# Hybrid attention layer: banded scores of two neighbouring pairs in one run, with the value sums in spare columns of the score tiles

## The chip, the cores and the metric

The kernel runs on one core of one Trainium2 chip. The metric is the device time of one execution in microseconds (us). A core has five engines that run their own instruction streams and wait for each other through semaphores: TensorE (PE; its weight loads are shown as PEld), VectorE (DVE), ScalarE (ACT), GpSimd (POOL) and SyncE (SP, which here only issues transfers). Matmul results go to PSUM, a small memory of eight banks. A bank holds 512 float32 columns in each of 128 partitions.

## The reference, cut to what matters

The reference is one decoder layer. A normalised input is projected to queries, keys, values and gates for two attention branches. Branch A is causal attention with a forget-gate bias over all 2048 positions. Branch B, the one that is changed here, is sliding-window attention with a window of 128 and a learned sink per head: eight query heads, two key/value heads, blocks of 128 queries. Each block sees the block of keys before its own and its own one.

```python
s = jnp.einsum('bnqhgd,bnshd->bnhgqs', qb, kk) * (d ** -0.5)
rel = i + Q_BLOCK - j
band = (rel >= 0) & (rel < WINDOW)
s = jnp.where(mask, s, -jnp.inf)          # mask = band, and no keys before block 0
p = jax.nn.softmax(jnp.concatenate([s, sink], axis=-1), axis=-1)[..., :-1]
out = jnp.einsum('bnhgqs,bnshd->bnqhgd', p, vv)
```

Both branches are gated, projected together, normalised and added to the residual. Inputs and output are float32, SEQ is 2048, D_MODEL 1024, a head 64 wide.

## The kernel before, in words

Every float32 product is made from float16 halves: a high and a low part on each side, and three matmuls (high·high, high·low, low·high) into the same PSUM columns.

The program has three long stages. First come the modulation, the normalised and transposed input and the first projections; then the banded branch B, which is worked off while the projections for both branches run; then branch A with the output projection. This case is about the second stage. Its PE stream is mostly projection matmuls, which are unit functions in a list (`punits`): three 512-column matmuls for a query or gate unit (L361), six 256-column ones for a value unit (L379). `fill(n)` emits the next n units.

Branch B has 32 `Pair` objects, the list `windows`: four pairs of heads (j) times eight pairs of query blocks (i = 0, 2, ... 14). They are called window 0 to 31 below. A pair goes through these parts:

- `scores` (L948): 12 matmuls on PE into a tile `pss` of two banks, one bank for each head. Each matmul contracts over 64 rows, half of the array; the two heads use the two halves. A bank has 256 columns for each of the two query blocks: 128 for the keys before, 128 for the block's own keys.
- `maxima` on DVE: L956 (COPY_PREDICATED) folds the first 128 columns of each 256 into the second 128, which works since within a band exactly one of the two is wanted at each place. L958 puts the sink into column 127. L961 and L963 make the row maximum and the bias.
- `exps` (L970): four exponentials on ACT, which read columns 127 to 255 of `pss`. After the fold, columns 0 to 126 of each 256 are read by nobody.
- `turn` (L977): four PE transposes into `pxb`; then L986 on ACT and L987 on DVE split the result into halves (`fold`), and four selections on POOL (L991, L993) unfold it into two weight tiles `ptb`.
- `pv` (L1005): 24 matmuls of 64 columns on PE (18 for i = 0), the sums of values, into a tile `pob` with a bank of its own. L1011 on DVE (`out_`) multiplies them by the reciprocal of the sums, and `o_store` sends them to memory.

The order in this stage is written by hand: every engine executes what the source calls, in the order of the calls. `after(k, f)` holds f back until the k-th `tick()` from there. Step n of the loop over windows reads: tick; maxima of window n; a quarter of the step's units; turn of window n-1; tick; exps of n; second quarter; tick; pv of n-2; third quarter; tick; last quarter; scores of n+1. A step is about 7.8 us. There is one `pss` buffer, so the scores of n+1 wait until the exps of n have read it.

PSUM in this stage: three banks `bk` for projections, two for `pss`, one for `pxb`, one for `pob`; the eighth is unused.

Of the kernel before, what the change touches and what calls it, by code (L numbers as in the profile page):

```python
# [10 lines left out]
F32 = mybir.dt.float32  # L11
# [5 lines left out]
ALU = mybir.AluOpType  # L17
AX = mybir.AxisListType

P = 128  # L20
# [4 lines left out]
CH = 512  # L25
# [18 lines left out]
def hybrid_layer(  # L44
# [17 lines left out]
    V, A, G, PE, SP = nc.vector, nc.scalar, nc.gpsimd, nc.tensor, nc.sync  # L62
# [5 lines left out]
    PSUM = bass.MemoryType.PSUM  # L68
# [14 lines left out]
    def sm(n, tag):  # L83
        return small.tile([P, n], F32, tag=tag, name=tag)
# [117 lines left out]
    def after(n, f):  # L202
        late.append([n, f])

    def tick():
        now = [f for n, f in late if n <= 1]
        late[:] = [[n - 1, f] for n, f in late if n > 1]
        for f in now:
            f()
# [85 lines left out]
    def o_store(on, pool, ci, rows_, cols_, eng, lag):  # L295
        if ci == 0:
            eng.dma_start(o_d[0][rows_, cols_].rearrange("(u p) c -> p u c", p=P), on)
            return
        u0, u1 = rows_.start // P, rows_.stop // P
        oh = pool.tile([P, u1 - u0, 2, on.shape[-1]], F16, tag="oh", name="oh")  # L300

        def low():
            V.tensor_tensor(oh[:, :, 1], on, oh[:, :, 0], op=ALU.subtract)
            eng.dma_start(o_d[ci][u0:u1, :, :, cols_].rearrange("u n p c -> p (u n) c"),
                          oh[:].rearrange("p u n c -> p (u n) c"))

        after(lag, lambda: A.activation(oh[:, :, 0], on, AF.Copy))
        after(lag + 1, low)
# [179 lines left out]
    with ExitStack():  # L488
# [114 lines left out]
        for _ in range(3):  # L603
            e = math.floor(math.log2(rest))
# [177 lines left out]
    def swa_pool(name, bufs, **kw):  # L782
        return swa.enter_context(tc.tile_pool(name=name, bufs=bufs, reuse_waits="tile", **kw))
# [148 lines left out]
    class Pair:  # L932
# [5 lines left out]
            self.blocks = [(i + e, max(i + e - 1, 0), 1 + min(i + e, 1)) for e in range(2)]  # L938

        def scores(self):  # L940
            self.pss = ps_s.tile([P, 2, CH], F32, tag="s", name="pss")
            q = ab[self.j, self.i // 4]
            for e, (i, k0, nk) in enumerate(self.blocks):
                qo, o = (i % 4) * P, e * 2 * P + (2 - nk) * P
                for n, (a, b) in enumerate(((0, 0), (0, 1), (1, 0))):
                    for h in range(2):
                        r = slice(64 * h, 64 * h + 64)
                        PE.matmul(self.pss[:, h, o:o + nk * P], q[r, a, qo:qo + P],  # L948
                                  kst[self.g][r, b, k0 * P:(i + 1) * P], start=(n == 0), stop=(n == 2))
# [45 lines left out]

            after(1, split)

        def pv(self):
            j, i = self.j, self.i
            po = ps_pv.tile([P, 4, 64], F32, tag="pv", name="pob")  # L1000
            for e, (i_, k0, nk) in enumerate(self.blocks):
                for h in range(2):
                    for b in range(nk):
                        for n, (pp_, vv) in enumerate(((0, 0), (0, 1), (1, 0))):
                            PE.matmul(po[:, 2 * e + h, :], self.ptt[b + 2 - nk][:, pp_, 2 * e + h, :],  # L1005
                                      vb[:, k0 + b, self.g, 64 * vv:64 * vv + 64],
                                      start=(b == 0 and n == 0), stop=(b == nk - 1 and n == 2))

            def out_():
                on = onp.tile([P, 2, P], F32, tag="on", name="on")  # L1010
                V.tensor_tensor(on[:].rearrange("p e (h d) -> p (e h) d", h=2), po[:],  # L1011
                                self.rinv[:].unsqueeze(2).broadcast_to([P, 4, 64]), op=ALU.mult)
                o_store(on[:], onp, i // 4, slice((i % 4) * P, (i % 4 + 2) * P), slice((4 + j) * P, (5 + j) * P), G, 1)

            after(1, out_)
# [166 lines left out]
    windows = [Pair(j, i) for j in range(4) for i in range(0, NB, 2)]  # L1182
    pos = [0]

    def fill(n, each=None):

        for _ in range(n):
            for f in events.pop(pos[0], []):
                f()
            punits[pos[0]]()  # L1190
            pos[0] += 1
            if each:
                each()
# [8 lines left out]
    with swa_order:  # L1202
        fill(N_PRO - 4, tick2)
        psx.close()
        sws = swa_pool("sws", 2)
        ptp = swa_pool("ptp", 1)
        ps_s = swa_pool("ps_s", 1, space=PSUM)
        ps_t = swa_pool("ps_t", 1, space=PSUM)
        ps_pv = swa_pool("ps_pv", 1, space=PSUM)
        wsp = swa_pool("wsp", 2)  # L1210
        wss, wst = sm(16, "a_m"), sm(2, "wst")
        wsq = {}
        base = N_PRO
        NW = len(windows)
        windows[0].scores()
        windows[0].maxima()
        fill(2, tick2)
        windows[0].exps()
        fill(2, tick2)
        for n, wd in enumerate(windows):  # L1220
            goal = base + (N_SWA - base) * (n + 1) // NW
            todo = goal - pos[0]
            part = [todo * (m + 1) // 4 - todo * m // 4 for m in range(4)]
            tick()
            if n:
                wd.maxima()
            fill(part[0])
            if n:
                windows[n - 1].turn()
            tick()  # L1230
            if n:
                wd.exps()
            fill(part[1])
            tick()
            if n > 1:
                windows[n - 2].pv()
            fill(part[2])
            tick()
            fill(part[3])
            if n + 1 < NW:  # L1240
                windows[n + 1].scores()

            if n:
                A.activation(wsq[n - 1][:], wsq[n - 1][:], AF.Square, accum_out=wss[:, (n - 1) % 16:(n - 1) % 16 + 1])
            if n == 16:
                V.tensor_reduce(wst[:, 0:1], wss[:], axis=AX.X, op=ALU.add)
            wsq[n] = wsp.tile([P, 2 * P], F32, tag="wsq", name="wsq")
            SP.dma_start(wsq[n][:], w_out0[n // 4 * P:(n // 4 + 1) * P, n % 4 * 2 * P:(n % 4 + 1) * 2 * P])
        tick()
        fill(5)  # L1250
        windows[NW - 1].turn()
        tick()
        fill(5)
        windows[NW - 2].pv()
        tick()
        fill(6)
        windows[NW - 1].pv()
        tick()
        tick()
        A.activation(wsq[NW - 1][:], wsq[NW - 1][:], AF.Square, accum_out=wss[:, 15:16])  # L1260
        V.tensor_reduce(wst[:, 1:2], wss[:], axis=AX.X, op=ALU.add)
        wsum = sm(1, "w_mx2")
        V.tensor_reduce(wsum[:], wst[:], axis=AX.X, op=ALU.add)
# [605 lines left out]
```

## Time and profile before

| | |
|---|---|
| median of three runs | 1130.42 us (1130.37 to 1131.12) |
| the profiled execution | 1129.92 us, its span from first to last instruction 1128.2 us |
| granted TensorE clock in it | 0.999 |
| PE matmuls busy | 1110.6 us, 98% of the span |
| DVE, ACT, POOL busy | 905.6, 656.8 and 224.6 us |
| scores of the 32 windows | first at 139.8 us, last at 378.9 us |

A matmul's busy time overlaps that of its neighbours, so two matmuls are compared by when they start. In the timeline a row merges instructions of one kind that follow each other: start, length from the first start to the last end, engine, line, operation, count; in square brackets stands the engine's idle time before the row and what ended it. A 512-column matmul takes 0.38 us from start to end, but the next one starts after 0.22 us. A view of windows gives the busy time of each engine in stretches of the span.

### The profile page before, as it was taken

To read this page: it belongs to the slowest core of one execution; us is meant where nothing else is said; L and a number is where in the kernel's file an instruction comes from. 1 tells how busy PE (TensorE), PEld (TensorE's weight loads), DVE (VectorE), ACT (ScalarE), POOL (GpSimd) and SP (SyncE) were. 2 spreads that over 40 slices of the span, in tenths; PEclk is the share of its full clock that TensorE was granted. 3 is DMA by queue.
4 is the path that set the end of the run, shared out by engine and by line. 5 is a ranking of instruction groups with operands and counts; after the bars stand their busy time and mean duration, and the time that the engine had idled before them with its cause. 6 is when DMAs were issued, how large, how long until landed. Compare 5 with 4: busy or idle time off the path is not lost.

```text
span 1128.2 us, 25138 instructions
## 1 busy us (share of the span) xinstructions
PE 1110.6 (98%) x9854; PEld 652.4 (58%) x9854; DVE 905.6 (80%) x1988; ACT 656.8 (58%) x1145; POOL 224.6 (20%) x343
## 2 busy tenths in 40 slices
PE   7899999999999999999999999999999999999997
PEld 2566555676756856556555555655556565544444
DVE  8897488878887468898998989988897997766663
ACT  3974345555555412666766667676666889543332
POOL 3111145545556420010010111001000000100000
PEclk9999999999999999999999999999999999999999
DMA  9854434413333142244223333224311245797632
GB/s 364 280 154 96 81 103 90 93 53 92 83 80 89 39 93 51 65 103 44 58 72 74 86 57 87 51 52 71 72 39 46 76 142 164 153 258 213 193 127 102
DMA packets 124653, 119.77 MB, mean 106 GB/s; under 512 B 66009, under 2 KB 102274, under 8 KB 124534
## 3 DMA queue, kind: packets, MB, share of 16 engines
q1 hardware_dynamic: 113662, 85.66, 28.4%
q0 software_dynamic: 10720, 32.46, 12.6%
q8 instruction: 77, 1.26, 0.6%
q14 instruction: 42, 0.34, 0.1%
q10 hardware_dynamic: 152, 0.04, 0.0%
HBM read 64.43 MB, written 25.18 MB: 79 GB/s over the span
## 4 chain that ended last, share of the span: by engine, by line
PE 83%; DVE 9%; DMA 3%; ACT 3%; issue 2%; SPq 0%; POOL 0%; DVEq 0%; POOLq 0%; ACTq 0%
PE bk L361 32%; PE bk L1650 14%; PE bk L379 7%; PE sta L1414 5%; PE sta L1415 5%; PE bk L1365 5%; PE poa L1440 3%; PE poa L1441 3%; PE poa L1438 3%; PE bk L854 2%; DMA wa<-in_w_ada_dram 2%; PE pss L948 2%; PE pob L1005 1%; PE px L453 1%; DMA xt<-in_x_dram 1%
## 5 line engine op out<-in xcount | busy, mean ns | idle before, releaser
L1421 ACT ACTIVATE p<-sta,lift,scl_qk 128x1024 f32<-128x1024 f32 (+2 forms) x160 | 171.8, 1074 | 128.1 <-PE sta L1415 78.9
L361 PE MATMUL bk<-hT,wh_qk 128*128 128x512 f16 x768 | 196.4, 378 | 0.0
L1428 DVE TENSOR_TENSOR pha<-p,pha 128x1024 f16<-128x1024 f32 (+2 forms) x160 | 168.9, 1056 | 0.2 <-ACT pha L1425 0.2
L1650 PE MATMUL bk<-wohl,oz 128*128 128x512 f16 x744 | 163.2, 379 | 0.0
L1368 DVE TENSOR_REDUCE a_m<-bk 128x1 f32<-128x512 f32 x192 | 130.1, 685 | 37.8 <-PE bk L1365 37.3
L1425 ACT ACTIVATE pha<-p 128x1024 f16<-128x1024 f32 (+2 forms) x160 | 147.8, 924 | 4.9 <-PE poa L1441 0.2
L1650 PEld LDWEIGHTS <-oz 128*128 128x128 f16 x744 | 71.0, 98 | 83.1
L1441 PE MATMUL poa<-vt,pha 128*128 128x65 f16 x1088 | 115.9, 192 | 0.7 <-DVE pha L1428 0.7
L1440 PE MATMUL poa<-vt,pha 128*128 128x64 f16 x1088 | 116.2, 194 | 0.0
L1438 PE MATMUL poa<-vt,pha 128*128 128x65 f16 x1088 | 116.2, 193 | 0.0
L361 PEld LDWEIGHTS <-wh_qk 128*128 128x128 f16 x768 | 71.8, 97 | 73.2 <-issue 1.3
L1414 PE MATMUL sta<-T 128*128 128x512 f16 (+1 forms) x320 | 110.9, 346 | 0.7 <-ACT p L1421 0.7
L1365 PE MATMUL bk<-T 66*128 66x512 f16 (+2 forms) x320 | 110.4, 348 | 0.5 <-DVE a_m L1368 0.2
L1415 PE MATMUL sta<-T 69*128 69x512 f16 (+1 forms) x320 | 109.8, 348 | 0.0
L1438 PEld LDWEIGHTS <-pha 128*128 128x128 f16 x1088 | 101.5, 96 | 14.3 <-issue 0.6
L1440 PEld LDWEIGHTS <-pha 128*128 128x128 f16 x1088 | 100.8, 97 | 11.4
L1441 PEld LDWEIGHTS <-pha 128*128 128x128 f16 x1088 | 100.9, 99 | 0.8 <-DVE pha L1428 0.8
L361 PE MATMUL bk<-hT,wh_za 128*128 128x512 f16 x384 | 100.4, 378 | 0.0
L361 PE MATMUL bk<-hT,wh_zb 128*128 128x512 f16 x384 | 92.1, 379 | 0.0
L379 PE MATMUL bk<-wh_va,hT 128*128 128x256 f16 x768 | 91.9, 273 | 0.0
L361 PE MATMUL bk<-hT,wh_qb 128*128 128x512 f16 x384 | 91.2, 379 | 0.0
L404 POOL DMA_DIRECT2D z_d<-tz x32 | 17.7, 555 | 342.5 <-DVE tz L402 250.9
(463 smaller groups left out, 1956.0 us busy)
## 6 DMA issues: line engine op xcount, KB each, us to landing
hT<-in_x_dram SPq DMA_DIRECT2D x20, 512.0 KB
wa<-in_w_ada_dram SPq DMA_DIRECT2D x16, 512.0 KB
z_d<-tz POOLq DMA_DIRECT2D x32, 256.0 KB, 3.1
T<-z_d SPq DMA_DIRECT2D x16, 512.0 KB
T<-stq SPq DMA_DIRECT2D x60, 128.0 KB
out_dram<-hT SPq DMA_DIRECT2D x15, 512.0 KB
xt<-in_x_dram SPq DMA_DIRECT2D x12, 512.0 KB
qs<-qf SPq DMA_DIRECT2D x80, 64.0 KB
```

The costliest lines, as they stand in the source:

```text
L361: PE.matmul(ps, whl[:, a, k, :], hT[ci][:, b, k, :], start=(k == 0 and n == 0), stop=(k == KT - 1 and n == 2))
L379: PE.matmul(ps[:, (u % 2) * 2 * P:(u % 2 + 1) * 2 * P], hT[ci][:, a, k, u * P:(u + 1) * P], wv[p][:, b, k, :], start=(k == 0 and n == 0), ...
L1365: PE.matmul(mx[:, :w], T[0:XM, 0, i * P:(i + 1) * P], T[0:XM, 2, pc * CH:pc * CH + w], start=True, stop=True)
L1414: PE.matmul(self.st[:, o:o + w], T[:, 3, kb_], T[:, 1, qc], start=True, stop=False)
L1415: PE.matmul(self.st[:, o:o + w], T[0:XR, 2, kb_], T[0:XR, 0, qc], start=False, stop=not diag)
L1421: A.activation(self.p32[:, :self.w], self.st[:, :self.w], AF.Exp, scale=scl[f"qk{self.hd}"][:], bias=lift[:])
L1425: A.activation(self.ph[:, 0, :self.w], self.p32[:, :self.w], AF.Copy)
L1428: V.tensor_tensor(self.ph[:, 1, :self.w], self.p32[:, :self.w], self.ph[:, 0, :self.w], op=ALU.subtract)
L1438: PE.matmul(po[:, u, :], ph[:, 0, pq], vt[:, b, hd, 0:65], start=(self.first and n == 0 and u == 0), stop=False)
L1440: PE.matmul(po[:, u, 0:64], ph[:, 0, pq], vt[:, b, hd, 65:VW], start=False, stop=False)
L1441: PE.matmul(po[:, u, :], ph[:, 1, pq], vt[:, b, hd, 0:65], start=False, stop=(self.last and n == len(self.blocks) - 1))
L1650: PE.matmul(py, self.hl[:, i, k, :], w_slot(8 * j + k)[:, cc], start=(k == 0 and m_ == 0), stop=(k == KT - 1 and m_ == 2))
```

## The change

There are two `pss` buffers, s0 and s1, of two banks each, and `pob` is gone: 3 + 4 + 1 banks, all eight. The windows take the buffers in the order s0, s1, s1, s0, s0, s1, s1, s0, and so on.

The scores of two windows are emitted together, 24 matmuls in one run: 0 and 1 before the loop, then n+1 and n+2 at the end of each odd step n. Even steps have no scores.

The value sums of window n-2 go to columns 0 to 63 of each 256 in a score tile ("home"). In an odd step this is the tile of window n-1, and `pv` stays where it was on PE but now stands ahead of the tick, so that `out_` comes a tick earlier. In an even step it is the tile of window n itself, and `pv` moves behind the third quarter of units. So the sums of windows n-2 and n-1 (n even) use the same tile one after the other, and the tile is next written by the scores of window n+3.

```diff
         def scores(self):
-            self.pss = ps_s.tile([P, 2, CH], F32, tag="s", name="pss")
+            self.pss = ps_s.tile([P, 2, CH], F32, tag=f"s{(self.i // 4 + self.i // 2) % 2}", name="pss")
...
-        def pv(self):
+        def pv(self, home):
             j, i = self.j, self.i
-            po = ps_pv.tile([P, 4, 64], F32, tag="pv", name="pob")
+            po = home.pss[:].rearrange("p h (e c) -> p e h c", e=2)[:, :, :, 0:64]
             for e, (i_, k0, nk) in enumerate(self.blocks):
...
-                            PE.matmul(po[:, 2 * e + h, :], self.ptt[b + 2 - nk][:, pp_, 2 * e + h, :],
+                            PE.matmul(po[:, e, h, :], self.ptt[b + 2 - nk][:, pp_, 2 * e + h, :],
...
             def out_():
                 on = onp.tile([P, 2, P], F32, tag="on", name="on")
-                V.tensor_tensor(on[:].rearrange("p e (h d) -> p (e h) d", h=2), po[:],
-                                self.rinv[:].unsqueeze(2).broadcast_to([P, 4, 64]), op=ALU.mult)
+                V.tensor_tensor(on[:].rearrange("p e (h d) -> p e h d", h=2), po,
+                                self.rinv[:].rearrange("p (e h) -> p e h", e=2).unsqueeze(3).broadcast_to([P, 2, 2, 64]),
+                                op=ALU.mult)
...
-        ps_pv = swa_pool("ps_pv", 1, space=PSUM)
...
         windows[0].scores()
+        windows[1].scores()
         windows[0].maxima()
...
             fill(part[1])
+            if n > 1 and n % 2:
+                windows[n - 2].pv(windows[n - 1])
             tick()
-            if n > 1:
-                windows[n - 2].pv()
             fill(part[2])
+            if n > 1 and n % 2 == 0:
+                windows[n - 2].pv(wd)
             tick()
             fill(part[3])
-            if n + 1 < NW:
-                windows[n + 1].scores()
+            if n % 2:
+                for wn in windows[n + 1:n + 3]:
+                    wn.scores()
...
-        windows[NW - 2].pv()
+        windows[NW - 2].pv(windows[NW - 2])
...
-        windows[NW - 1].pv()
+        windows[NW - 1].pv(windows[NW - 1])
```

Three places show how instructions move. The first is on PE at the end of step 3, where before the scores of window 4 end. L361 rows are projection units; in square brackets stand the engines whose semaphore is waited for. Before:

```order
L948 LDWEIGHTS stb
L948 MATMUL pss<-kst_576,stb 128x256
L361 LDWEIGHTS wh_qb_2115
L361 MATMUL bk_137<-hT_107,wh_qb_2115 128x512
L361 LDWEIGHTS wh_qb_2115
```

And with the change:

```order
L948 LDWEIGHTS stb
L948 MATMUL pss<-kst_576,stb 128x256
L948 LDWEIGHTS stb
L948 MATMUL pss<-kst_576,stb 128x256 [waits DVE_49]
L948 LDWEIGHTS stb
```

The scores of window 5 follow those of window 4 without a projection between. Their first matmul waits for DVE: for the L1011 of window 1, whose sums lie in the tile that window 5 now writes.

The second place is on PE in step 4, at the value sums of window 2 (weights `ptb`). Before:

```order
L361 LDWEIGHTS wh_qb_2115
L361 MATMUL bk_137<-hT_107,wh_qb_2115 128x512
L1005 LDWEIGHTS ptb [waits Pool_49]
L1005 MATMUL pob<-vb,ptb 128x64 [waits DVE_49]
L1005 LDWEIGHTS ptb
```

And with the change:

```order
L361 LDWEIGHTS wh_zb_1923
L361 MATMUL bk_139<-hT_108,wh_zb_1923 128x512
L1005 LDWEIGHTS ptb [waits DVE_49,Pool_49]
L1005 MATMUL pss<-vb,ptb 128x64 [waits Activation_49]
L1005 LDWEIGHTS ptb
```

Six L361 matmuls that stood behind the sums stand ahead of them. The first sum waits for ACT: for the last exponential of window 4, which reads the same tile. All even steps have this wait.

The third place is on DVE in step 5, around the L1011 of window 3. L285 is a weight split that waits for ACT; minus rows are of before, plus rows of the change:

```order
 L987 TENSOR_TENSOR fold<-pxb,fold 128x512
 L989 RECIPROCAL b_ri<-b_rs 128x4
-L285 SCALAR_TENSOR_TENSOR wh_va_2441<-wr_va_1990,w_sw,wh_va_2441 128x4x128
-L1011 TENSOR_TENSOR on<-pob,b_ri 128x256
-L285 SCALAR_TENSOR_TENSOR wh_va_2441<-wr_va_1990,w_sw,wh_va_2441 128x4x128
-L179 TENSOR_SCALAR kap_va_2490<-w_pw,pH 128x1
+L1011 TENSOR_TENSOR on<-pss,b_ri 128x256
+L285 SCALAR_TENSOR_TENSOR wh_va_2435<-wr_va_1987,w_sw,wh_va_2435 128x4x128 x2
+L179 TENSOR_SCALAR kap_va_2484<-w_pw,pH 128x1
+L303 TENSOR_TENSOR oh<-on,oh 128x2x128
```

L1011 now stands ahead of the first L285. In steps 7 and 9 it moves ahead of its neighbours in the same way; in step 3 it stays where it was. Behind the second stage the order of every engine is unchanged.

## The prediction

> **What bounds the kernel now.** I read the page first, then PE's timeline around one group of scores, then DVE and ACT at the places where the change puts waits.
>
> ```profile
> span 1128.2 us, 25138 instructions
> PE 1110.6 (98%) x9854; PEld 652.4 (58%) x9854; DVE 905.6 (80%) x1988; ACT 656.8 (58%) x1145; POOL 224.6 (20%) x343
> 160.00:170.00 10.00, 10.00 (x89) 5.34 (x85) 9.63 (x24) 4.73 (x14) 4.61 (x8) 1.00 0.31 89
> 170.00:180.00 10.00, 10.00 (x87) 5.24 (x86) 9.72 (x24) 5.67 (x21) 7.30 (x10) 1.00 0.45 107
> 240.00:250.00 10.00, 10.00 (x109) 7.47 (x106) 5.36 (x13) 4.37 (x15) 3.17 (x5) 1.00 0.18 53
> ```
>
> PE sets the end: 98% of the span, and 10.00 of 10 us in the windows of the banded stage. Whatever PE saves or waits there moves the rest of the program one for one, as PE has hardly any idle time later that could absorb it. The third number in a window row is DVE. It is full from 160 to 180 us (9.63, 9.72) and half empty at 240 us (5.36): a wait on DVE means different things early and late in the stage.
>
> **What merging the groups saves.** PE at the scores of window 4, from the merged timeline and from two narrow ones:
>
> ```profile
> 169.28 2.11 PE L361 MATMUL bk<-hT,wh_qb 128*128 128x512 f16 x9
> 171.32 0.83 PE L948 MATMUL pss<-kst,stb 64*128 64x256 f16 x12
> 171.32 0.39 PE L948 MATMUL pss<-kst,stb 64*128 64x256 f16 x4
> 171.66 0.49 PE L948 MATMUL pss<-kst,stb 64*128 64x256 f16 x6
> 172.08 1.47 PE L361 MATMUL bk<-hT,wh_qb 128*128 128x512 f16 x6
> 173.39 0.60 PE L977 MATMUL pxb<-ident,sm__2192 128*128 128x128 f32 x4
> ```
>
> Six L361 from 172.08 to 173.39 are 0.218 us apiece, so the nine from 169.28 would hand over at 171.23; the scores start at 171.32: entry costs about 0.10. The two heads of a pair run side by side. Four matmuls span 0.39 and six span 0.49, so a pair follows a pair after 0.10 to 0.11. The last of the three pairs from 171.66 then starts at about 171.87, and PE would go on at 171.98; L361 starts at 172.08: exit costs 0.10. A merged group drops one entry and one exit, 0.19 with the rounding. 32 groups become 16: **16 × 0.19 = 3.0 us saved**.
>
> Two groups waited besides:
>
> ```profile
> 206.34 2.75 PE L361 MATMUL bk<-hT,wh_zb 128*128 128x512 f16 x12
> 209.19 0.83 PE L948 MATMUL pss<-kst,stb 64*128 64x256 f16 x12
> 337.73 1.89 PE L361 MATMUL bk<-hT,wh_qb 128*128 128x512 f16 x8
> 339.73 0.83 PE L948 MATMUL pss<-kst,stb 64*128 64x256 f16 x12
> ```
>
> 12 × 0.216 from 206.34 and the entry give 209.03; the start at 209.19 is 0.16 late, at 339.73 likewise 0.17. The first is window 9, which now writes a tile that is free early: **0.16 saved**. The second is window 26, below. Matmuls, DVE, ACT and POOL instructions are otherwise the same in number and size, so they cost nothing more; one L1011 still reads 256 elements. SP's issues stand in the same order, and POOL only swaps five output stores with a neighbour; no engine waits for those stores in this stage.
>
> **New wait 1: window 5 on DVE's L1011 of window 1.** The chain on DVE that leads to it:
>
> ```profile
> 156.33 0.70 DVE L956 COPY_PREDICATED pss<-dmask,pss 128x512 f32<-128x512 int16 x1 [0.99 <-PE pss L948]
> 160.51 2.12 DVE L822 TENSOR_TENSOR qs<-qs,sinT 128x512 f32<-128x512 f32 x1
> 173.00 0.41 DVE L1011 TENSOR_TENSOR on<-pob,b_ri 128x256 f32<-128x256 f32 x1
> 184.78 0.17 DVE L989 RECIPROCAL b_ri<-b_rs 128x4 f32<-128x4 f32 x1
> 186.91 0.78 DVE L285 SCALAR_TENSOR_TENSOR wh_va<-wr_va,w_sw,wh_va 128x512 f16<-128x512 f32 x1 [1.97 <-ACT wh_va L278]
> 187.62 0.41 DVE L1011 TENSOR_TENSOR on<-pob,b_ri 128x256 f32<-128x256 f32 x1
> ```
>
> No row between 156.33 and 184.78 has idle time ahead of it: DVE works without a break. It starts when window 2's scores are there, now 0.19 earlier, so its L1011 ends at 173.41 - 0.19 = 173.22. PE gets to window 5 at 171.32 less two merges (0.38) plus window 4's six pairs (0.64): 171.58. **PE stands 1.6 us.** Behind it stand all projections, and nobody else has the work to fill. From below: if DVE loses L822's long 2.12 (a normal one is 0.69, see 191.19 in the next fence), 0.2. From above 2.1, if DVE is held again by the later turn.
>
> By the Trainium skill's page "SBUF — State Buffer" (section "SBUF: two separate sides"), a DVE instruction with two SBUF inputs and a GpSimd instruction lock each other out for the whole instruction. By that rule L822 is long since POOL's selections of window 1 run then; the trace agrees:
>
> ```profile
> 161.45 0.62 POOL L993 TENSOR_SCALAR_AFFINE_SELECT ptb<-fold 128x512 f16<-128x512 f16 x1
> 162.66 0.69 DVE L823 TENSOR_TENSOR qc<-qc,qs 128x512 f32<-128x512 f32 x1
> 191.19 0.69 DVE L822 TENSOR_TENSOR qs<-qs,sinT 128x512 f32<-128x512 f32 x1
> ```
>
> POOL's last selection ends at 162.07, and L822 at 162.63, one length later. The turn of window 1 moves behind window 3's scores, 0.45 later in all, and POOL with it, so I keep the long L822 and the 1.6.
>
> In steps 5, 7 and 9 the same wait (windows 7, 9, 11) finds DVE done: the L1011 moves ahead of L285, out of the ACT wait of 1.97, and runs near 185.4 instead of 187.62, while PE comes after 187. Later DVE has slack.
>
> **New wait 2: the sums of even steps on the exps of the same step.** First where PE leads, step 12:
>
> ```profile
> 234.70 0.60 PE L977 MATMUL pxb<-ident,sm__3165 128*128 128x128 f32 x4
> 235.14 1.46 PE L361 MATMUL bk<-hT,wh_qb 128*128 128x512 f16 x6
> 236.43 0.86 PE L1005 MATMUL pob<-vb,ptb 128*128 128x64 f16 x24
> 235.39 0.60 ACT L986 ACTIVATE fold<-pxb 128x512 f16<-128x512 f32 x1 [2.69 <-PE pxb L977]
> 235.88 0.45 ACT L970 ACTIVATE sm__3296<-pss,b_nb,scl_qb 128x129 f32<-128x129 f32 x1
> 237.53 0.22 ACT L970 ACTIVATION_READ_ACCUMULATOR sm__3296<-pss,b_nb,scl_qb 128x1 f32 x1
> ```
>
> ACT's exps stand behind L986, which waits for PE's turn at 234.70: they end at 237.75, 3.05 after it. The sums stood 1.73 after the turn; with six more L361 (1.30) they stand 3.03 after it. PE arrives 0.02 early, plus some 0.05 for the signal: 0.07 a step. About ten even steps from 10 to 30 are built like that: **0.7 us**; from 0 to 1.2.
>
> Early, where DVE is late, steps 4, 6 and 8:
>
> ```profile
> 177.93 0.21 ACT L970 ACTIVATION_READ_ACCUMULATOR sm__2311<-pss,b_nb,scl_qb 128x1 f32 x1
> 190.14 0.86 PE L1005 MATMUL pob<-vb,ptb 128*128 128x64 f16 x24
> 192.95 0.21 ACT L970 ACTIVATION_READ_ACCUMULATOR sm__2552<-pss,b_nb,scl_qb 128x1 f32 x1
> ```
>
> Step 6: PE at 190.14 + 1.30 (units) + 0.64 (window 7's scores, already done) - 0.57 (three merges) + 1.6 (the stall above) = 193.1; the exps end at 193.16 less what DVE gains. The stall above has paid for most of this; I take **0.5 us** for the three steps together, 0 to 1.9 if DVE in turn is held by the later sums.
>
> The Trainium skill, "PSUM — Partial Sum Buffer" (section "PSUM bank collisions raise a hardware error"), wants PSUM guarded by bank, not by address. That speaks against the change: the columns are free after the fold, yet their bank is busy until the exps have read it. The built order agrees, as the sums wait for ACT. If only the columns counted, this wait would end with DVE's fold and its 1.2 us would be 0.
>
> **Window 26.** DVE is full here again:
>
> ```profile
> 325.57 0.27 DVE L955 MEMSET pss<- 128x256 f32 x1 [1.62 <-PE pss L948]
> 339.47 0.20 ACT L970 ACTIVATION_READ_ACCUMULATOR sm__4947<-pss,b_nb,scl_qb 128x1 f32 x1
> ```
>
> From the start on window 24's scores, DVE and ACT need until 339.67 for the exps of 25, which window 26 waits for. PE cannot use its merge there: its 0.17 wait becomes 0.36, which costs **0.2** of what I booked as saved; 0 to 0.7.
>
> **Sum:** -3.0 - 0.16 + 1.6 + 0.7 + 0.5 + 0.2 = -0.2 us. The profiled execution took 1129.92 (1.7 outside its span), so 1129.7; the median of the runs is 0.5 above it: **1130.2 us**. With all waits at their lower ends (0.2, 0, 0, 0) it would be 1127.5; with all at their upper ends (2.1, 1.2, 1.9, 0.7) 1133.1.
>
> **Rivals.**
> - The gain stays (0.18). DVE reaches L1011 by 171.6, and the exps of steps 4 to 8 are earlier as well. Terms: -3.16 + 0.2 + 0.4 (half the 0.7) = -2.6, so 1127.8. For it: L1011 moves ahead in many steps, and L822's 1.4 us may go. Against it: without a stall at window 5, step 6's sums would meet exps that end 1.6 later than PE comes, so DVE would have to gain twice.
> - Slower (0.13). DVE executes in order, and L1011 of an even step is now called right behind sums that PE reaches about 2 us later than before. DVE then stands, and the next maxima, exps and scores are late. Before, the list of waits has it three times:
>
> ```profile
> DVE on L1011 <- PE pob L1005: 3.7, 3, 1.7
> ```
>
> In the seven even steps where DVE is full (4 to 10, 20, 24, 26), 0.7 each would be 4.9. Half of it in PE's way, on top of the sum, gives about 1132.7; it decides from about 0.7 a step. Against it: after the stall at window 5 DVE has slack.
> - The change does not save what it says (0.05): the 0.19 belongs to something else than the change of shape. Then +3.0 on the sum, 1133.2. Against it: entry and exit look the same at every group.
>
> **How the numbers follow.** My forecast, stalls eating nearly all of the gain, has 0.64, with its own range 1128.6 to 1131.9. A measurement of this kernel tells about 0.2% from no change, 2.3 us: faster is below 1128.2, slower above 1132.7. The first rival lies mostly beyond the one border, half of the second and most of the third beyond the other, and the forecast's own tails reach a little over both. Faster 0.19, same 0.68, slower 0.13. The range for 8 in 10 is 1128.0 to 1132.5.
>
> **What would show it.** The stage's end on PE before:
>
> ```profile
> 401.01 0.28 PE L1722 MATMUL bk<-w_mx,ones 128*128 128x1 f32 x2
> ```
>
> Right: 16 runs of 24 score matmuls, each with one entry and one exit; one PE wait of 1 to 2 us at about 171.6 on DVE L1011; waits of up to 0.1 on ACT L970 ahead of the sums of even steps; total PE matmul idle up by some 3 us in the stage. L1722 would come within 1 us of 401.01. Wrong: no wait at 171.6, or even-step waits of 0.3 and more after 230 us, or DVE rows of L1011 with a microsecond of idle time ahead of them.

## The result and the profile after

The change made the kernel slower: 1137.63 us median (1135.05 to 1139.78) against 1130.77 (1130.04 to 1131.81) for the kernel before on the same chip, a ratio of 1.0061 with a 95% interval of 1.0044 to 1.0077. That is 6.9 us, outside the range of the prediction. The profiled execution of the changed kernel, 1139.78 us, is the longest of its runs; the one of before, 1129.92 us, is shorter than each of the six of this comparison. So the profiles lie 9.9 us apart, 3.0 more than the medians.

Nearly all of it arises in the banded stage. The page of the changed kernel, two of its windows with one of before between them (columns as in the prediction: length, busy time of PE, PEld, DVE, ACT and POOL, granted clock, share of the transfer engines, GB/s), and PE's timeline with the first two long stalls, a merged run, and the end of the stage, which stood at 401.01 us before:

```profile
span 1138.1 us, 25131 instructions
PE 1111.5 (98%) x9854; PEld 655.9 (58%) x9854; DVE 905.1 (80%) x1988; ACT 656.9 (58%) x1145; POOL 221.9 (20%) x343
```

```profile
170.00:180.00 10.00, 8.49 (x80) 4.74 (x79) 8.79 (x22) 4.39 (x17) 7.28 (x10) 1.00 0.35 102
280.00:290.00 10.00, 10.00 (x109) 8.30 (x108) 7.04 (x20) 6.15 (x19) 5.82 (x9) 1.00 0.40 65
280.00:290.00 10.00, 8.60 (x86) 5.71 (x84) 5.99 (x12) 4.15 (x15) 5.20 (x9) 1.00 0.40 50
```

```profile
173.25 0.83 PE L948 MATMUL pss<-kst,stb 64*128 64x256 f16 x12 [1.51 <-DVE on L1011]
...
194.98 0.86 PE L1005 MATMUL pss<-vb,ptb 128*128 128x64 f16 x24 [1.59 <-ACT sm__2558 L970]
...
236.40 1.48 PE L948 MATMUL pss<-kst,stb 64*128 64x256 f16 x24
237.81 1.47 PE L361 MATMUL bk<-hT,wh_qb 128*128 128x512 f16 x6
...
410.24 0.28 PE L1726 MATMUL bk<-w_mx,ones 128*128 128x1 f32 x2
```

The stage ends 9.2 us later and the span is 9.9 longer; past the stage there is little to find. The merging is there as forecast: at 236.40 us 24 score matmuls stand in one row, with one entry and one exit. PE, which was full in these windows before (the middle row above and those of the prediction), is now idle for 1.5 us of 170 to 180 us and for 1.4 us of 280 to 290. What it waited for, from the list of PE's waits between 135 and 411 us (total, times, longest):

```profile
PE pss L1005 <- ACT sm__4329 L970: 2.3, 1, 2.3
PE pss L1005 <- ACT sm__2558 L970: 1.6, 1, 1.6
PE pss L948 <- DVE on L1011: 1.5, 1, 1.5
PE pss L1005 <- ACT sm__2805 L970: 1.4, 1, 1.4
PE pss L1005 <- ACT sm__4036 L970: 1.4, 1, 1.4
PE pss L948 <- ACT sm__4921 L970: 0.9, 1, 0.9
```

The kernel before has no row of PE in this list at all. Counted as start-to-start distance above the usual one, which includes the signal, these are: step 20 2.48 us, step 6 1.76, window 5 1.68, step 8 1.59, step 18 1.57, window 26 0.94. Eight even steps add 0.07 to 0.10 each, together 0.7, and two small ones (window 21, the sums in step 26) 0.6. Behind the longest stall PE ran 3.4 us at half its clock, which cost 1.35 us. The sum is some 12.6; less the 3.0 saved and the 0.34 that PE had stood before, 9.3, where the stage's end shows 9.2.

### The profile page after: what moved, and what is told of

It is laid out like the page before. It is cut to its first block, busy times and chain, and to the rows that moved or that the text cites. A ratio compares the mean times of both kernels' runs of the same rounds, so it can differ in the third digit from the quotient of the medians.

```text
span 1138.1 us, 25131 instructions
## 1 busy us (share of the span) xinstructions
PE 1111.5 (98%) x9854; PEld 655.9 (58%) x9854; DVE 905.1 (80%) x1988; ACT 656.9 (58%) x1145; POOL 221.9 (20%) x343
## 4 chain that ended last, share of the span: by engine, by line
PE 79%; DVE 9%; DMA 5%; ACT 3%; issue 3%; POOL 1%; SPq 0%; DVEq 0%; POOLq 0%; ACTq 0%
PE bk L361 31%; PE bk L1654 13%; PE bk L379 5%; PE sta L1418 5%; PE sta L1419 5%; PE bk L1369 4%; PE poa L1444 3%; PE poa L1445 3%; PE poa L1442 3%; PE bk L854 2%; DMA wa<-in_w_ada_dram 2%; PE pss L1005 1%; PE pss L948 1%; PE px L453 1%; DMA mxr<-mx_d 1%
## 5 line engine op out<-in xcount | busy, mean ns | idle before, releaser
L361 PE MATMUL bk<-hT,wh_qk 128*128 128x512 f16 x768 | 196.4, 378 | 0.0
L361 PEld LDWEIGHTS <-wh_qk 128*128 128x128 f16 x768 | 71.8, 97 | 73.2 <-issue 1.3
L361 PE MATMUL bk<-hT,wh_za 128*128 128x512 f16 x384 | 100.4, 378 | 0.0
L361 PE MATMUL bk<-hT,wh_qb 128*128 128x512 f16 x384 | 91.7, 384 | 0.0
L361 PE MATMUL bk<-hT,wh_zb 128*128 128x512 f16 x384 | 91.4, 379 | 0.0
```

Source lines behind the costliest of these rows:

```text
L361: PE.matmul(ps, whl[:, a, k, :], hT[ci][:, b, k, :], start=(k == 0 and n == 0), stop=(k == KT - 1 and n == 2))
```

## The experiments

The first theory: PE stands because sums of even steps now need the exps of the same step and window n+3's scores need an L1011. Its rivals: the merging itself costs; the late transfers that the second half of the profile shows (ACT's L1248 stands for 5.8 us there) are the cause, whatever PE waits for; DVE and ACT are simply the bound in these steps, so that a stall that is removed comes back elsewhere.

| kernel | median, us | ratio to before (95%) | stage's end in its profile, us | PE's extra gaps, us |
|---|---|---|---|---|
| changed kernel, again | 1136.25 | 1.0051 (1.0036 to 1.0065) | 406.78 | 9.1 |
| scores singly | 1140.94 | 1.0089 (1.0076 to 1.0102) | 412.40 | 11.7 |
| both sums in odd steps | 1135.79 | 1.0048 (1.0036 to 1.0060) | 408.77 | 10.6 |
| the same, window 5 alone | 1135.88 | 1.0038 (1.0026 to 1.0049) | 405.69 | 8.2 |
| sums in pairs | 1129.97 | 1.0000 (0.9991 to 1.0008) | 400.44 | 2.6 |
| the change without squares | 1134.32 | 1.0040 (1.0027 to 1.0053) | 404.81 | 7.5 |
| before without squares | 1130.32 | 0.9999 (0.9990 to 1.0008) | 401.00 | 0.4 |
| pairs, tiles in turn | 1129.52 | 0.9994 (0.9985 to 1.0003) | 399.85 | 2.1 |
| the same, scores singly | 1132.49 | 1.0018 (1.0009 to 1.0027) | 402.25 | 0.9 |
| pairs split by the turn | 1128.91 | 0.9985 (0.9976 to 0.9994) | 400.10 | 2.1 |

The last two columns are of one profiled execution each, which is not the median one (that of "both sums in odd steps" took 1138.61 us). The last column sums what the distances between PE's matmuls have above the usual ones, from 130 to 420 us; excesses below 0.06 us are not counted, those of matmuls at a low clock are (1.6 us in "scores singly", 2.8 in "both sums in odd steps", none in the others of the table). It is 12.6 in the first profile of the change and 0.3 in that of the kernel before.

**The changed kernel again.**

> The changed kernel once more, so that its stalls are seen in a second execution. Waits theory (PE stands at the sums of even steps, which now need the exps of the same step, and at window 5's scores, which need an L1011): the stalls of 1.7 us at window 5 and of about 1.7 us each at the sums of steps 6 and 8 return in every execution, and the time stays 4 to 9 us above the kernel before. Transfer theory (the loss is in late transfers of qs, wsq and mxr around 283 to 294 us, by accident of one execution): the stalls of steps 18 and 20 and the low clock at 307 us are gone here or stand elsewhere, and the time follows them by up to 5 us.

Measured: 1136.25 us. Window 5 (1.68), step 6 (1.75) and step 8 (1.59) are the same to 0.01 us, and so is window 26 (0.94). Steps 18 and 20 shrink from 1.57 and 2.48 to 1.1 each, and there is no low clock. So the first group belongs to the kernel, and what varies between executions are the transfers behind steps 18 and 20 and the clock.

**Scores singly.**

```diff
-        windows[1].scores()
...
-            if n % 2:
-                for wn in windows[n + 1:n + 3]:
-                    wn.scores()
+            if n + 1 < NW:
+                windows[n + 1].scores()
```

> Two tiles and the sums in their columns as in the change, but the scores of one window at the end of every step, as before. Waits theory: the 3.0 us of merging are lost, the stall of 1.7 us at window 5 goes, and the sums of even steps stand longer for it (steps 4, 6 and 8 together by 1 to 2 us more): 1137 to 1141 us. Rival, the merging itself costs (a group of 24 score matmuls holds PE while DVE waits for the maxima of the even window): without it the time falls back to 1130 to 1133 us.

Measured: 1140.94 us, in the range of the waits theory; the merging is not what costs. The stage ends 2.2 us later than in the first profile of the change (412.40 against 410.24), although PE's extra gaps are 0.9 smaller (11.7 against 12.6): without the merging 3.1 us are missing, as the prediction has it. With no stall at window 5, the sums of step 4 stand (first row; the second is step 6):

```profile
PE pss L1005 <- ACT sm__2306 L970: 1.3, 1, 1.3
PE pss L1005 <- ACT sm__2545 L970: 0.9, 1, 0.9
```

**Both sums in odd steps.** The sums of window n-3 stand at the start of odd step n, those of n-2 at their old place, both in the tile of n-1. The new second argument of `pv` is the first column of each 256.

```diff
+            if n > 2 and n % 2:
+                windows[n - 3].pv(windows[n - 1])
             tick()
...
-                windows[n - 2].pv(windows[n - 1])
+                windows[n - 2].pv(windows[n - 1], 64)
...
-            if n > 1 and n % 2 == 0:
-                windows[n - 2].pv(wd)
```

> As the change, but both sums of two steps in the odd step: those of window n-3 at its start and of n-2 at their old place, side by side in the free columns of window n-1, whose exps ended a step ago. Waits theory: the waits on L970 ahead of sums are gone (about 3.4 us at steps 6 and 8, 4.0 at 18 and 20, 0.7 of small ones), with them the low clock; window 5's 1.7 us stays, and some 0.3 and 0.9 us at windows 21 and 26: 1130.8 - 3.0 - 0.2 + 2.9 = 1130.5 us, 1129 to 1132. Transfer theory: the stalls around 287 and 305 us come whatever PE waits for, at another instruction: 1134 to 1137 us.

Measured: 1135.79 us. The first theory falls in its simple form: the waits of the even steps are gone, the loss is not. The sums in the next step still meet exps that are not done, and the second sums now wait for the L1011 of the first:

```profile
PE pss L1005 <- DVE on L1011: 2.9, 2, 2.2
PE pss L948 <- DVE on L1011: 1.9, 1, 1.9
PE pss L1005 <- ACT sm__2805 L970: 1.3, 1, 1.3
PE pss L1005 <- ACT sm__4329 L970: 1.0, 1, 1.0
```

The number is what the transfer theory gave, but of the five stalls behind these rows three (172, 212 and 340 us) are far from the late transfers.

**Window 5 alone.** In the last kernel, window 5 is scored at the end of step 4.

```diff
-                for wn in windows[n + 1:n + 3]:
+                for wn in windows[n + 1:n + 2 + (n != 3)]:
                     wn.scores()
+            if n == 4:
+                windows[5].scores()
```

> As the kernel with both sums in the odd step, and window 5's scores alone at the end of step 4, so that they need not wait for the L1011 of window 1. Waits theory: 1.7 us less of stall, one merge less (0.2): 1.5 us below the kernel with both sums in the odd step, so 1129.0 us, 1127.5 to 1130.5. Rival, the stall only paid for later ones (PE meets late exps or late maxima at windows 6 to 9 instead): no difference of more than 0.5 us between the two.

Measured: 1135.88 us, no better. The stall of 2.06 us that the kernel above has at window 5 is gone, and the sums of window 3 stand for 1.94 us in step 5 instead (from 181.66), for an L1011. This is the rival's case: as long as the next meeting of PE with DVE or ACT has as little slack, it takes over the stall.

**Sums in pairs.** The second theory: DVE and ACT run up to some 2.5 us behind in steps 4 to 9 and 18 to 26, also in the kernel before; PE stands wherever the order gives it less slack than that. So both sums go next to each other, with no L1011 between them, where the exps they need were called four quarters of a step earlier (the expectation below says three, but by the order of the calls it is four; in the change it is two, for the scores of the kernel before three).

```diff
             fill(part[0])
+            if n > 2 and n % 2:
+                windows[n - 3].pv(windows[n - 1])
+                windows[n - 2].pv(windows[n - 1], 64)
             if n:
                 windows[n - 1].turn()
...
-            if n > 1 and n % 2:
-                windows[n - 2].pv(windows[n - 1])
...
-            if n > 1 and n % 2 == 0:
-                windows[n - 2].pv(wd)
```

> As the change, but the sums of windows n-3 and n-2 stand one behind the other in odd step n, after its first quarter and ahead of the turn, in the columns 0 to 63 and 64 to 127 of window n-1's tile, with no L1011 between them; both L1011 follow at once. PE needs the exps of step n-1 three quarters of a step after they are issued, where the change needed them within a quarter, and the L1011 of window n-2 stands a quarter of a step earlier on DVE. Slack theory (DVE and ACT run up to 2.5 us behind in steps 4 to 9 and 18 to 26, as before, and PE stands wherever it needs their result with less slack than that): no PE wait ahead of L1005, window 5's wait under 1 us, about 0.9 left at window 26, so 1130.8 - 3.0 - 0.2 + 1.5 = 1129.1 us, 1128 to 1131. Rival (DVE and ACT are now the bound themselves in these steps, so that the same 8 us of standing come back at another place): 1134 us or more.

Measured: 1129.97 us. That is 6.3 us below the changed kernel, or 5.5 when each is set against the kernel before on its own chip; the gaps fall from 9.1 to 2.6. The wait of window 5 is gone, but two waits ahead of L1005 remain (0.79 and 0.24 us), where I expected none. DVE does the same work (905.9 us busy) and stands longer for PE than in the changed kernel:

```profile
PE pss L948 <- ACT sm__2454 L970: 0.8, 1, 0.8
PE pss L1005 <- ACT sm__2805 L970: 0.6, 1, 0.6
PE pss L948 <- ACT sm__4945 L970: 0.6, 1, 0.6
...
DVE on L1011 <- PE pss L1005: 8.0, 6, 2.5
```

In the first profile of the changed kernel the last of these rows reads 5.6 us. So DVE's standing behind late sums, the second rival of the prediction, is not the loss by itself, and neither are DVE and ACT the bound: with slack, PE goes on.

**Without the squares.** ACT's L1248 squares pieces of `w_out`, which SP's queue brings as `wsq`. Both are left out and their sums set to 1 (so the scale of the output projection is not computed), in the change and in the kernel before.

```diff
+        V.memset(wss[:], 1.0)
...
-                A.activation(wsq[n - 1][:], wsq[n - 1][:], AF.Square, accum_out=wss[:, (n - 1) % 16:(n - 1) % 16 + 1])
...
-            wsq[n] = wsp.tile([P, 2 * P], F32, tag="wsq", name="wsq")
-            SP.dma_start(wsq[n][:], w_out0[n // 4 * P:(n // 4 + 1) * P, n % 4 * 2 * P:(n % 4 + 1) * 2 * P])
```

> The change without the squares of w_out's pieces: ACT's L1248 and the wsq transfers ahead of it on SP's queue are left out and their sums set to 1 (this part of the computation is missing). Transfer theory: with no 128 KB piece on the queue at 277 us, qs lands on time, DVE's L822 and ACT do not stand, and the stalls of steps 18 and 20 (1.1 to 1.6 and 1.1 to 2.5 us) and the low clock go: 1132 to 1134 us. Slack theory: those of window 5 and of steps 6 and 8 stay at 1.6 to 1.8 us each, whatever becomes of 18 and 20. If the late transfers have another cause, the stalls of 18 and 20 stay as well: 1135 to 1138 us.

> The kernel before without the same squares and transfers, as the measure for the change without them: PE has no idle time of more than 0.4 us in its banded stage, so nothing to win: 1130.0 to 1131.2 us under each theory.

Measured: 1134.32 and 1130.32 us. The kernel before does not care. In the change, steps 18 and 20 stand 0.25 and 0.22 us in place of 1.1 and 1.1 (or 1.57 and 2.48), and the clock stays up; the list of PE's waits has the others unchanged:

```profile
PE pss L1005 <- ACT sm__2542 L970: 1.6, 1, 1.6
PE pss L948 <- DVE on L1011: 1.5, 1, 1.5
PE pss L1005 <- ACT sm__2783 L970: 1.4, 1, 1.4
PE pss L948 <- ACT sm__4848 L970: 0.9, 1, 0.9
```

So the stalls of steps 18 and 20 hang on the squares and their transfers: between the second profile of the change and this one they lose 1.7 us, and in the first, with the clock, some 5 hung on them. By the medians the gain is not clear of noise: 1.9 us between the two, 1.2 when each is set against its own kernel before, and the intervals of the two ratios overlap. The rest of the loss, all early stalls among it, stays. Not all went as the transfer theory had it: DVE's L822 still stands 1.92 us for `qs` (2.48 in the second profile), so `qs` is late without the squares too. What is gone is ACT's wait for the square's piece (4.42 us) and DVE's for another small transfer, `mxr` (1.25). The kernel leaves out ACT's squares (0.42 us each) together with the transfers, so it does not separate the two.

**Pairs, tiles in turn.** In the kernel with pairs window 6 and window 26 were the first of their merged runs and overwrote the tile whose exps were just being read. With the tiles in turn it is the second.

```diff
-            self.pss = ps_s.tile([P, 2, CH], F32, tag=f"s{(self.i // 4 + self.i // 2) % 2}", name="pss")
+            self.pss = ps_s.tile([P, 2, CH], F32, tag=f"s{self.i // 2 % 2}", name="pss")
```

> As the kernel with the sums in pairs, with the two tiles taken in turn (even windows one, odd windows the other). Of the two windows that are scored at the end of odd step n, it is then the second that overwrites window n and waits for its exps, 0.64 us later on PE than the first. Slack theory: the waits of 0.82 us at window 6 and of 0.67 us at window 26 shrink to 0.2 and 0, those of 0.8 and 0.24 us at L1005 stay: about 1.2 us below the kernel with pairs, 1128.8 us (1128 to 1129.6), and PE's extra gaps between 130 and 420 us fall from 2.6 to 1.3 us. If the first window now meets a late L1011 instead, the sum of the gaps stays at 2.6 and the time at 1130.

Measured: 1129.52 us. Both waits shrink as expected (0.17 us and none). Since PE comes sooner, the second sums now meet POOL's selections at 196 and 303 us, 0.57 and 0.60 us above the usual distance, and the gaps fall to 2.1, not to the 1.3 expected:

```profile
PE pss L1005 <- POOL ptb L993: 0.8, 2, 0.4
```

**The same, scores singly**, with the edit shown above.

> The kernel with pairs and the tiles in turn, with the scores of one window at the end of every step, as before: the change without merging, and with no wait for the exps of the same step. It measures what merging alone saves. By the 0.19 us a merge: no extra gap on PE of more than 0.4 us, 1130 to 1130.8 us, so no faster than the kernel before, and the kernel with pairs and merging lies 3.0 us less its own gaps below it. If merging saves nothing, both are within 0.5 us of each other less the gaps, so this one 1 us faster.

Measured: 1132.49 us, 2.97 above the kernel with merged scores. That kernel has 1.2 us more of gaps, so merging alone is worth 3.6 us by the stage's ends (402.25 - 399.85 + 1.2), where the first such pair of kernels gave 3.1. It does save what the prediction said, or somewhat more. The kernel also is 2 us slower than the kernel before, where I expected none. At the stage's end it is 1.2: 0.6 us of that are gaps, and 0.5 are transposes, since the first of the four takes 0.143 us to the next start and not 0.109 where it follows the sums directly, as it does 15 times in every kernel with pairs. The remaining 0.8 lie past the stage, where the profiled executions of this case differ by up to 1.1 us.

**Pairs split by the turn.** The turn between the two sums gives POOL 0.6 us more. The last line of the edit keeps DVE's order as it was.

```diff
                 windows[n - 3].pv(windows[n - 1])
-                windows[n - 2].pv(windows[n - 1], 64)
             if n:
                 windows[n - 1].turn()
+            if n > 2 and n % 2:
+                windows[n - 2].pv(windows[n - 1], 64)
...
-            after(1, out_)
+            late.insert(len(late) - (o > 0), [1, out_])
```

> As the kernel with pairs and the tiles in turn, with the turn of window n-1 between the two sums of odd step n; DVE's order is the same to the instruction. The sums of window n-2 stand 0.6 us later on PE, and by that much their wait for POOL's L993 shrinks (0.57 and 0.60 us at 196 and 303 us). Slack theory: PE's extra gaps fall from 2.1 to 1.0 us and the time from 1129.5 to 1128.4 us (1127.8 to 1129.4). If DVE, whose second L1011 and fold now come after the turn, is late next, the gaps return at window 6 or 26 and the time stays at 1129.5.

Measured: 1128.91 us, ratio 0.9985 (0.9976 to 0.9994): 1.4 us faster than the kernel before, and some 7 faster than the change. In its profile, of one of its longer executions (1129.45 us), the wait for POOL at 196 us is 0.10, but the one at 303 us still 0.79. The expected fall of the gaps to 1.0 did not come, and its step from the kernel with the tiles in turn (0.6 us) is inside the spread of both. That this order beats the kernel before the change is measured; which of its terms does it is not.

## Why the prediction was wrong

**Right, with its size:** the merging (3.0 us forecast; 3.1 and 3.6 by the two pairs of kernels with and without it, and 16 runs of 24), window 5's stall (1.6 forecast, 1.68 measured, on the L1011 named), the small waits where PE leads (0.07 forecast, 0.07 to 0.10 measured in eight steps, 0.7 in all), and that DVE, ACT and PE have no other work to do. Window 5's size is in part luck: L1011 ended at 173.21 us as forecast (173.22), but DVE stood 0.62 us for the later turn on the way, and L822 took 1.47 us, not the 2.12 that I kept, because POOL's selections came 0.2 us earlier and not later. The two cancel, since L822 ends 0.56 us after POOL's last selection both times (its normal length, by which I read it, is 0.69).

**Wrong: the sums of steps 4, 6 and 8.** "The stall above has paid for most of this; I take 0.5": it measured 3.35 us (1.76 in step 6, 1.59 in step 8), above even the upper end of 1.9. I held DVE's and ACT's times of before fixed, less what DVE gains, and let PE come later. PE came as forecast: its last unit before the sums started at 193.01 us, so they could have started at 193.2. The exps of window 6 were the term that failed: they ended at 194.92 us, where I had 193.16 less what DVE gains. The stall holds DVE and ACT too. DVE in steps 4 to 6 of the kernel before, then of the changed kernel, then ACT of the changed kernel:

```profile
176.14 0.68 DVE L987 TENSOR_TENSOR fold<-pxb,fold 128x512 f16<-128x512 f32 x1
176.83 0.65 DVE L822 TENSOR_TENSOR qs<-qs,sinT 128x512 f32<-128x512 f32 x1
...
182.06 0.68 DVE L956 COPY_PREDICATED pss<-dmask,pss 128x512 f32<-128x512 int16 x1
...
191.02 0.23 DVE L963 TENSOR_SCALAR b_nb<-b_m,nscl_qb 128x4 f32<-128x4 f32 x1
```

```profile
176.64 0.69 DVE L987 TENSOR_TENSOR fold<-pxb,fold 128x512 f16<-128x512 f32 x1 [0.93 <-ACT fold L986]
177.33 1.12 DVE L822 TENSOR_TENSOR qs<-qs,sinT 128x512 f32<-128x512 f32 x1
...
183.02 0.69 DVE L956 COPY_PREDICATED pss<-dmask,pss 128x512 f32<-128x512 int16 x1
...
189.75 0.41 DVE L303 TENSOR_TENSOR oh<-on,oh 128x256 f16<-128x256 f32 x1
...
192.33 0.69 DVE L963 TENSOR_SCALAR b_nb<-b_m,nscl_qb 128x4 f32<-128x4 f32 x1
```

```profile
186.70 1.15 ACT L278 ACTIVATE wh_va<-wr_va,w_sw 128x1024 f16<-128x1024 f32 x1
...
193.06 0.46 ACT L970 ACTIVATE sm__2558<-pss,b_nb,scl_qb 128x129 f32<-128x129 f32 x1 [1.55 <-DVE b_nb L963]
...
194.72 0.20 ACT L970 ACTIVATION_READ_ACCUMULATOR sm__2558<-pss,b_nb,scl_qb 128x1 f32 x1
```

PE's stall puts the turn of window 3 late (175.33 us, before 173.39), so L986, and DVE's L987 stands 0.93 us for it where it had not stood before. With a longer L822 behind it (1.12 us, before 0.65), the maxima of window 5 start at 183.02 us instead of 182.06, ACT's weight split L278 that follows the exps of 5 moves along, L285 on DVE waits for that, and L285 runs 0.97 us late. L303, which the earlier L1011 brings ahead of the maxima of window 6 (it came behind them before, at 192.53), adds 0.33, and L963, which takes 0.69 us over a selection on POOL instead of 0.23, another 0.46. So the exps of window 6 end 1.8 us late. Of these, 0.50 are DVE's stand for the turn, and so the stall itself; 0.47 and 0.46 are two DVE instructions that now meet POOL's selections at other places; 0.33 is the changed order, which took back what DVE gained by the earlier L1011. The stall bought PE 1.6 us and DVE and ACT lost 1.8. The one-sided sum "PE's arrival less their end" holds only as long as nothing in between waits for PE and nothing on DVE changes its length. Step 8 I have not followed in this way.

**Wrong: steps 18 and 20, which I counted at 0.07 each.** They measured 4.05 us in the first profile and 2.1 in the second. ACT, of the changed kernel:

```profile
285.74 0.42 ACT L1248 ACTIVATE wsq<-wsq 128x256 f32<-128x256 f32 x1 [5.79 <-DMA wsq<-in_w_out_dram]
...
288.80 0.21 ACT L970 ACTIVATION_READ_ACCUMULATOR sm__4036<-pss,b_nb,scl_qb 128x1 f32 x1
```

The exps of window 18 stand behind a square of the output weights, whose piece comes 6 us late; DVE's L822 waits for `qs` from the same queue at that time (2.97 us), and ahead of step 20 its L255 for `mxr` (3.00 us, before 0.36). In the kernel before neither `qs` nor this piece is waited for at this place. That the stalls of steps 18 and 20 hang on the squares and their transfers is shown by the kernel without them. But a late piece alone does not make a stall. In the kernel with pairs ACT waits for the same piece as well, and 4.25 us in the kernel split by the turn, and PE does not stand for those exps:

```profile
280.56 0.42 ACT L1247 ACTIVATE wsq<-wsq 128x256 f32<-128x256 f32 x1 [3.20 <-DMA wsq<-in_w_out_dram]
```

So this loss, too, looks like one of slack: here two quarters of a step did not cover a late piece, and four did. Part of the lateness is that DVE asks for `qs` 4.3 us after its last issue, where it was 5.9 before; why the transfers take longer as well I could not settle. In the row of before that I read for all late even steps (step 12) nothing waits for a transfer.

**Wrong: window 26**, 0.2 forecast, 0.94 measured. L822 and POOL's first selection of before, then DVE and POOL of the changed kernel:

```profile
330.27 0.96 DVE L822 TENSOR_TENSOR qs<-qs,sinT 128x512 f32<-128x512 f32 x1
330.67 1.04 POOL L991 TENSOR_SCALAR_AFFINE_SELECT ptb<-fold 128x512 f16<-128x512 f16 x1
```

```profile
338.69 3.20 DVE L822 TENSOR_TENSOR qs<-qs,sinT 128x512 f32<-128x512 f32 x1
```

```profile
338.94 0.65 POOL L991 TENSOR_SCALAR_AFFINE_SELECT ptb<-fold 128x512 f16<-128x512 f16 x1
339.54 0.64 POOL L993 TENSOR_SCALAR_AFFINE_SELECT ptb<-fold 128x512 f16<-128x512 f16 x1
340.12 0.63 POOL L991 TENSOR_SCALAR_AFFINE_SELECT ptb<-fold 128x512 f16<-128x512 f16 x1
340.71 0.63 POOL L993 TENSOR_SCALAR_AFFINE_SELECT ptb<-fold 128x512 f16<-128x512 f16 x1
```

This L822 took 0.96 us before. Now it meets the four selections of POOL and ends 0.55 us after the last of them. DVE has no idle time from there to the L963 of window 25, which the exps that window 26 needs wait for; from the start of L822 to that L963 it takes 1.1 us more than before, not 2.2, as the instructions behind L822 now lose less to POOL. I kept such a collision for step 3 and did not look for new ones. It costs where slack is missing: in the kernel with pairs L822 takes 3.20 us too and window 26 waits 0.67, and with the tiles in turn, again 3.20, it does not wait.

**Not foreseen: the clock**, 1.35 us in the first profile and nothing in the second; see below.

**The rivals.** The slower one had the right sign and the wrong mechanism: DVE does stand more at L1011 (5.6 us, eight times, before 3.7, three times), but the kernel with pairs has 8.0 us of it and no loss. What decides is slack in PE's way. The prediction's own sign of error, "even-step waits of 0.3 and more after 230 us", came true.

## What to carry to other kernels

A dependency that is new on the bounding engine should be weighed by its slack in the worst step, not by its wait in a typical one: here a quarter of a step (some 1.9 us) of slack on ACT's exps was given up, in six places PE then stood 0.9 to 2.5 us, and the loss was some 10 us where the gain was 3. A stall does not pay in full for the next one when the engines it would let catch up wait for the stalled engine themselves. Removing such waits one by one (two kernels here) moved the loss; putting the sums a whole step behind the exps removed most of it, and the gain of the merging appeared.

## What the runs showed of the hardware

**A short stall can cost PE its clock.** The granted clock (the third column from the end) behind step 20's stall in the changed kernel, where no matmul started between 304.53 and 307.23 us, and in the kernel with window 5 alone, none between 338.63 and 340.88:

```profile
307.00:308.00 1.00, 0.77 (x20) 0.77 (x20) 0.96 (x4) 0.57 (x4) 0.96 (x1) 0.78 0.00 0
308.00:309.00 1.00, 1.00 (x10) 0.53 (x8) 1.00 (x3) 0.00 (x0) 1.00 (x2) 0.50 0.08 16
309.00:310.00 1.00, 1.00 (x4) 0.38 (x3) 1.00 (x4) 0.18 (x1) 1.00 (x2) 0.50 0.00 0
310.00:311.00 1.00, 1.00 (x4) 0.38 (x3) 0.93 (x3) 0.24 (x1) 0.16 (x1) 0.52 0.23 29
311.00:312.00 1.00, 1.00 (x8) 0.63 (x7) 0.88 (x3) 0.28 (x1) 0.00 (x0) 1.00 0.82 193
```

```profile
341.00:342.00 1.00, 1.00 (x26) 0.78 (x25) 0.93 (x3) 0.77 (x2) 0.16 (x1) 1.00 0.60 96
```

At 0.50 a 512-column matmul follows the other after 0.43 us in place of 0.22, for 3.41 us (307.55 to 310.96). Four distances had such a stretch behind them (2.70 here, 2.45 in the kernel with single scores, 2.17 and 2.59 in the one with both sums in odd steps); four did not (2.19 in the kernel with single scores; 2.16, 2.25 and 2.30 in the one with window 5 alone), and none below 2.0 did. So between 2.17 and 2.30 us the length alone does not decide. The place in time has a part in it. Within one profile the drops, and the clock's first rise near the start, lie whole multiples of 3.413 us apart: 87 from 10.59 to 307.55 us here, 49 from 175.32 to 342.57 in the kernel with both sums in odd steps. All four stalls with a drop lie inside one such period, counting from the modelled end of the last matmul, and the clock drops when the period ends; two of the four others (2.16 and 2.25) are cut by the end of a period. The other two are not, so more than this decides. The Trainium skill, "TensorE: Matmul & The Clock Gate" (section "Why this matters for your kernels"), warns of idle gaps above about 3 us; here 2.17 us between two starts (1.90 of them idle by the modelled ends) was enough once, so the measurement decides.

**DVE can lose more than one instruction's length to POOL.** L822, which reads two SBUF tiles, took 3.20 us over four selections in a row; the 2.12 us of the prediction are such a case too, with three selections behind its start. In the kernel before, in the rows shown at window 26, it took 0.96 and the selections 1.04 to 1.07 each. By the starts of the rows L822 was first in both, by 0.25 and by 0.40 us, so what decides which engine loses stays open. The Trainium skill, "SBUF — State Buffer" (section "SBUF: two separate sides"), speaks of a lock for one whole instruction; in the rows of the changed kernel DVE did not get in between POOL's four.
